# Transposed output projection with router logits beside it, first expert started after half a gather, and one-block weight tiles first in the ring

## The chip, the core and the metric

The kernel runs on one core of a Trainium2 chip. The metric is the device time of one execution in microseconds (us), taken as the median of several runs. Traces and pages of the profile come from one execution recorded by the hardware profiler.

## The reference

One transformer block on 256 tokens of width 1024, all in float32. A mixer (a gated linear recurrence, a differential attention and a sliding-window attention, merged by gates) is followed by a mixture of 32 experts, of which each token takes 4. The part that matters here runs from the merged mixer output to the first expert:

```python
merged = jnp.einsum('bsnd,bsnd->bsd', gates, branch_proj)
return merged @ w_out                                   # output projection, 1024 x 1024
...
x = x + g_m * hybrid_mixer(h, ...)                      # residual
h = rms_norm(x, norm_ffn[layer]) * (1.0 + sc_f) + sh_f
...
logits = xt.astype(jnp.float32) @ w_router.astype(jnp.float32) + b_router.astype(jnp.float32)
top_v, top_e = lax.top_k(logits, TOP_K)
weights = jax.nn.softmax(top_v, axis=-1).astype(xt.dtype)
...
def expert_block(args):
    tok, e = args
    hcat = x_pad[tok] @ w1[e] + b1[e]                   # 1024 -> 2048
    ...
    return act @ w2[e] + b2[e]                          # 1024 -> 1024
```

The weights of the 32 experts are 32 x 12 MB; everything else that is read is small beside them.

## The kernel before

**Stages.** The mixer's branches come first, then `merge` (L621), `project` (L671, the product with `w_out`), `route` (L721, logits, top 4, ranks of the tokens within each expert), and `moe` (L1092), which loops over the experts. An expert takes the tokens chosen for it (at most 64) as columns: `gather` (L865) makes, for four experts at a time, the 1024 x 256 tile `xT` by products of the scaled residual with a one-hot matrix `sel`; `up` (L916) multiplies `xT` by `w1`; `activate`, `down` (L932) and `scatter` follow. The order is up(0), then for each next expert up(e), activate(e-1), down(e-1).

**Weights.** All weights pass through a ring of tiles that SyncE (SP) loads in program order. A *block* is 128 x 2048 float32, 1 MB; the ring of the expert stage has 16 blocks in ten tiles: u0, u1, u2, v0, v1, v2 of two blocks, u3, w0, w1, w2 of one. `slot` (L69) takes the next tile in the list `self.order`; `blocks` (L87) fills a two-block tile by one DMA (L92) and a pair of one-block tiles by two (L96 and L84). A tile is loaded again when the products that read it have ended. While `project` runs, v1, v2 and w2 still hold `w_out`. The order of the ring is set in `mixer`:

```python
self.order = [(wp3, f"u{i}", 2) for i in range(3)] + [o["v0"], o["v1"], (wp3, "u3", 1)] \
    + [o[t] for t in ("w1", "w2", "w0", "v2")]
```

So up(0), which reads eight blocks k = 0..7, reads u0, u1, u2, v0.

**Precision.** The products up to `project` are made of three fast float32r products (`mm3`, L121: high x high, high x low, low x high); `split` (L111) makes the two parts of 128 x 1024 of a weight block, the high one on ScalarE (ACT, L117), the low one on VectorE (DVE, L109), in three buffers. Logits, transposes and expert products are plain float32.

**project and route_half.** `project` makes the output rows by tokens: the merged tile `m` is the stationary operand, `w_out` moves, 512 columns at a time; 48 products for each half of the 1024 columns. DVE multiplies by the row tile `gmB` (the mixer gate copied to all partitions by 8 products at L669) and adds to `x`. `route_half` (L699) then squares `x` on ACT for the norm, transposes the half of `x` by 8 PE transposes, copies it to `x1T`, and multiplies it by the router weights (four products of 32 output partitions each, L718). `route` brings the logits back to tokens (L727), scales them by the norm (`rs`), finds the top 4 (L743 to L748), counts by products with triangular ones (L750 to L754) and gets `rank` (L756). `scaled` (L761) makes the high and low part (`xs`) of the normed x, the low part half on DVE, half on ACT and GpSimd (POOL).

**gather.** For each of 8 chunks d of 128 channels: four products of 128 x 256 (two token halves, high and low part, L883) into one half of a PSUM bank, then DVE (even d) or ACT (odd d) scales the result into `xT`.

Two more things move in the change: the row tile `gf` (the second gate, 8 products, made in `project`) and `counts` (L791), whose result `cnti` SP reads into a register (L1022) ahead of the loads that follow in its order.

The order on each engine is made by a list scheduler from the program text; DMA issues are in one SP queue. The engines wait on semaphores.

## Time and profile before

| what | value |
|---|---|
| median of 3 runs | 1236.9 us (1235.44 to 1237.43) |
| the profiled execution | 1238.5 us, of which the span from first to last instruction is 1236.7 us |
| granted TensorE clock, mean | 0.983 of full |
| busy: PE, DVE, ACT, POOL | 1125.8 us (91%), 452.7 us (37%), 259.3 us (21%), 11.0 us (1%) |
| DMA | 470.70 MB, mean 381 GB/s over the span; 414 to 429 GB/s in each slice from 310 us to 1175 us |

How to read it: the span has a first part of some 300 us (mixer and routing) in which PE, DVE and the loads take turns at the limit, and an expert part in which the loads run at one rate almost to the end. Busy shares over the whole span mix the two. A row of the timeline gives start, duration, engine, source line, operation, tiles written and read, and how many instructions are merged in the row; a float32 product shows as two records.

### The profile page before, as it was taken

How to read it: one execution, taken by the hardware profiler on the slowest of the kernel's cores; microseconds unless marked ns; L12 is line 12 of the kernel's file. 1: busy time of each engine (PE TensorE's matmuls, PEld its weight loads, DVE VectorE, ACT ScalarE, POOL GpSimd, SP SyncE). 2: the span in 40 equal slices, each digit the busy share in tenths (PEclk: the TensorE clock that was granted, in tenths of full speed). 3: DMA queues.
4: the chain of work that ended last, by engine and by line, in shares of the span. 5: the costliest groups of instructions: out<-in, count | busy, mean ns of one | idle time of the engine just before them, and what ended most of it. 6: DMA issues, size and time to landing. Idle time of an engine off the chain costs nothing.

```text
span 1236.7 us, 13932 instructions
## 1 busy us (share of the span) xinstructions
PE 1125.8 (91%) x5719; PEld 552.4 (45%) x5720; DVE 452.7 (37%) x892; ACT 259.3 (21%) x446; POOL 11.0 (1%) x19
## 2 busy tenths in 40 slices
PE   5998999998988999998989798979898989798987
PEld 4787989995333334332323242324233323332333
DVE  3477888974123231231213132403131222121232
ACT  4475668444101011100000010101010100100000
POOL 0000000000010000000000000000000000000000
PEclk9998999998999999999999999999999999999999
DMA  9688467885999999999999999999999999999996
GB/s 376 210 288 299 147 218 264 343 325 219 414 417 425 424 424 426 427 426 425 423 429 424 429 424 424 429 424 424 423 427 427 424 426 424 427 426 426 423 403 237
DMA packets 54718, 470.70 MB, mean 381 GB/s; under 512 B 6048, under 2 KB 8152, under 8 KB 21112
## 3 DMA queue, kind: packets, MB, share of 16 engines
q1 hardware_dynamic: 53112, 466.93, 91.9%
q0 software_dynamic: 528, 1.72, 0.4%
q10 hardware_dynamic: 1008, 1.09, 0.3%
q8 instruction: 47, 0.77, 0.3%
q14 instruction: 23, 0.19, 0.0%
HBM read 468.65 MB, written 1.07 MB: 380 GB/s over the span
## 4 chain that ended last, share of the span: by engine, by line
PE 55%; DMA 41%; DVE 2%; ACT 1%; issue 1%; SPq 0%; DVEq 0%; ACTq 0%
DMA wt<-w2h 31%; PE po L923 10%; PE mm L923 9%; PE ps L943 7%; DMA wt<-w1h 7%; PE ps L956 3%; PE mm L124 3%; PE mm L125 3%; PE mm L126 3%; PE ps L883 3%; DMA wada<-wada 2%; PE ps L850 1%; PE po L125 1%; PE po L126 1%; PE po L124 1%; PE ps L420 1%
## 5 line engine op out<-in xcount | busy, mean ns | idle before, releaser
L923 PE MATMUL po<-wt,xT 128*64 128x512 f32 x992 | 335.7, 599 | 29.1 <-DMA wt<-w1h 29.1
L923 PE MATMUL mm<-wt,xT 128*64 128x512 f32 x992 | 331.4, 594 | 0.0
L943 PE MATMUL ps<-wt,act 128*64 128x512 f32 x992 | 234.3, 614 | 43.0 <-DMA wt<-w2h 36.1
L949 DVE TENSOR_TENSOR y<-ps,gf 64x512 f32<-64x512 f32 x62 | 42.7, 689 | 352.2 <-PE ps L943 351.5
L923 PEld LDWEIGHTS po<-wt,xT 128*64 128x64 f32 x992 | 87.8, 136 | 169.3 <-issue 112.7
L943 PEld LDWEIGHTS ps<-wt,act 128*64 128x64 f32 x992 | 72.7, 140 | 190.0 <-issue 133.6
L923 PEld LDWEIGHTS mm<-wt,xT 128*64 128x64 f32 x992 | 93.0, 137 | 132.5 <-issue 130.8
L853 DVE TENSOR_TENSOR g<-ps,b1t 128x512 f32<-128x512 f32 x31 | 21.4, 691 | 242.9 <-PE ps L850 242.9
L109 DVE TENSOR_TENSOR wlo<-wt,whi 128x1024 fp32r<-128x1024 f32 x72 | 85.6, 1192 | 35.6 <-ACT whi L117 34.4
L117 ACT CAST whi<-wt 128x1024 fp32r<-128x1024 f32 x72 | 73.5, 1023 | 74.4 <-PE ps L126 27.7
L927 ACT COPY hg<-po 128x512 f32<-128x512 f32 x31 | 18.1, 585 | 302.3 <-PE po L923 256.2
L126 PE MATMUL mm<-h,wlo 128*128 128x256 f32 x256 | 73.7, 288 | 0.0
L125 PE MATMUL mm<-h,whi 128*128 128x256 f32 x256 | 73.5, 287 | 0.0
L124 PE MATMUL mm<-h,whi 128*128 128x256 f32 x256 | 73.4, 287 | 0.0
L856 ACT ACTIVATE ps<-g 128x512 f32<-128x512 f32 x31 | 18.6, 601 | 219.9 <-DVE g L854 219.9
L956 PE MATMUL ps<-y,swT 128*128 128x512 f32 (+1 forms) x128 | 58.2, 606 | 6.4 <-DVE y L949 6.4
L958 DVE TENSOR_TENSOR x<-x,ps 128x512 f32<-128x512 f32 x64 | 43.8, 687 | 18.9 <-PE ps L956 18.9
L124 PEld LDWEIGHTS mm<-h,whi 128*128 128x128 f32 x256 | 49.1, 192 | 1.4 <-issue 1.3
L125 PEld LDWEIGHTS mm<-h,whi 128*128 128x128 f32 x256 | 49.0, 191 | 1.1 <-issue 1.0
L126 PEld LDWEIGHTS mm<-h,wlo 128*128 128x128 f32 x256 | 49.0, 192 | 1.0 <-issue 1.0
L886 ACT ACTIVATE xT<-ps,B,A 128x256 f32<-128x256 f32 x32 | 17.3, 564 | 139.1 <-PE ps L883 138.7
L206 DVE CUSTOM_DVE_ANT_0 wada<-wada,silu,cols 128x1024 f32<-128x1024 f32 x32 | 40.8, 1275 | 7.8 <-DMA wada<-wada 7.8
(335 smaller groups left out, 1103.7 us busy)
## 6 DMA issues: line engine op xcount, KB each, us to landing
wt<-w1h SPq DMA_DIRECT2D x93, 2048.0 KB, 29.5
wt<-w2h SPq DMA_DIRECT2D x47, 2048.0 KB, 29.5
wt<-w1h SPq DMA_DIRECT2D x70, 1024.0 KB, 29.6
wt<-w2h SPq DMA_DIRECT2D x33, 1024.0 KB, 31.3
wt<-wch SPq DMA_DIRECT2D x16, 1024.0 KB, 6.7
wada<-wada SPq DMA_DIRECT2D x32, 512.0 KB, 4.7
wada<-wad SPq DMA_DIRECT2D x16, 512.0 KB, 9.4
wt<-wqkv SPq DMA_DIRECT2D x8, 896.0 KB, 8.7
```

The source lines that it names most:

```text
L109: eng.tensor_tensor(lo, x, hi.bitcast(F32), op=ALU.subtract)
L117: self.nc.scalar.copy(hi, w)
L124: nc.tensor.matmul(out, lhs[0], rhs[0], start=start, stop=False)
L125: nc.tensor.matmul(out, lhs[0], rhs[1], start=False, stop=False)
L126: nc.tensor.matmul(out, lhs[1], rhs[0], start=False, stop=stop)
L206: nc.vector.tensor_tensor_reduce(out=w, in0=w, in1=self.csb, scale=0.5, scalar=self.col(C_BADA + c), op0=ALU.mult, op1=ALU.add, accum_out= ...
L883: nc.tensor.matmul(p[:, i * 256:(i + 1) * 256], self.xs[j][:, t, d * 128:(d + 1) * 128], sel[:, t], start=(t + j == 0), stop=(t + j == 2))
L923: nc.tensor.matmul(p[64 * hf:64 * hf + 64], xT[:, k, i * CAP:(i + 1) * CAP], w[:, (2 * j + hf) * 512:(2 * j + hf + 1) * 512], start=(k == ...
L943: nc.tensor.matmul(py[rows[hf]], act[:, (k % 4) * 2 + k // 4, :], w[:, (2 * i + hf) * 512:(2 * i + hf + 1) * 512], start=(k == 0), stop=(k ...
L949: nc.vector.tensor_mul(self.y[r, hf], py[r], self.gf[r, hf * 512:(hf + 1) * 512])
L956: nc.tensor.matmul(p, swT[r, i, t * 128:(t + 1) * 128], self.y[r, hf], start=True, stop=True)
L958: nc.vector.tensor_add(self.x[:, t, s], self.x[:, t, s], p)
```

## The change

1. `project` makes the output transposed: `w_out` (laid out anew) is the stationary operand and `m` moves, 256 columns (the tokens) at a time, in 8 chunks of 128 channels with 24 products each. Before each pair of chunks x is transposed (4 transposes, L687 of the new file) and copied to `x1T`; DVE adds the gated chunk to it in one instruction (L698); each chunk has its own logit product (L699). The sum is transposed back (4 for a pair, L704), squared on ACT straight from PSUM (L706) and copied to `x` by DVE (L707). The row tile `gmB` is gone.
2. The low part of the scaled x (`rest`) is made by DVE alone, in four instructions issued behind the one-hot tiles; ACT makes only the four high parts. The weights of the chosen experts (`route_weights`), `counts` and `gf` come behind up(0) in the program.
3. `gather` yields after each pair of chunks. For the first group up(0) runs on PE in the order written: two pairs, blocks k = 0 and 1, a pair, k = 2 and 3, the last pair, the other blocks. The results of the first gather are all scaled by ACT.
4. The ring begins with the one-block tiles w1 and w2: up(0) reads w1, w2, u0, u1, u2.

```diff
@@ mixer
-            self.order = [(wp3, f"u{i}", 2) for i in range(3)] + [o["v0"], o["v1"], (wp3, "u3", 1)] \
-                + [o[t] for t in ("w1", "w2", "w0", "v2")]
+            self.order = [o["w1"], o["w2"]] + [(wp3, f"u{i}", 2) for i in range(3)] \
+                + [o["v0"], o["v1"], (wp3, "u3", 1), o["w0"], o["v2"]]
@@ router_weights
-        self.gmB = self.row_tile("gmB", gm, self.keep2)
@@ project
-        for hf in range(2):
-            s = slice(hf * 512, (hf + 1) * 512)
-            ps = self.proj([self.mm(), self.mm()], m, self.a["wout"][hf])
-            if hf == 0:
-                self.route_open(st)
-            else:
-                self.gf = self.row_tile("gf", self.mod[:, 40:48], self.keep, self.mm)
-            for t in range(2):
-                y = self.keep2.tile([128, 512], F32, name="y", tag="gb", bufs=2)
-                nc.vector.tensor_mul(y, ps[t], self.gmB[:, s])
-                nc.vector.tensor_add(self.x[:, t, s], y, self.x[:, t, s])
-            self.route_half(hf)
...
+        for i, w in enumerate(self.blocks([self.a["wout"][hf] for hf in range(2)])):
+            b = slice(256 * i, 256 * (i + 1))
+            pt = self.ps()
+            for c in range(2):
+                for t in range(2):
+                    nc.tensor.transpose(pt[:, c * 256 + t * 128:c * 256 + (t + 1) * 128],
+                                        self.x[:, t, b.start + c * 128:b.start + (c + 1) * 128], self.ident)
+            nc.scalar.copy(x1T[i], pt.rearrange("p (c m) -> p c m", c=2))
+            p = self.mm()
+            for c in range(2):
+                d, q = 2 * i + c, slice(c * T, (c + 1) * T)
+                hi, lo = self.split(w[:, c * 1024:(c + 1) * 1024])
+                for k in range(8):
+                    s = slice(k * 128, (k + 1) * 128)
+                    self.mm3(p[:, q], (hi[:, s], lo[:, s]), (m[0][:, k], m[1][:, k]), k == 0, k == 7)
+                xT = x1T[i][:, c]
+                nc.vector.scalar_tensor_tensor(xT, p[:, q], self.gm[:, d:d + 1], xT, op0=ALU.mult, op1=ALU.add)
+                nc.tensor.matmul(self.plg[32 * (d % 4):32 * (d % 4) + 32, :T], self.wr[:, d, :], xT,
+                                 start=(d < 4), stop=(d >= 4))
+            pb = self.ps()
+            for t in range(2):
+                for c in range(2):
+                    nc.tensor.transpose(pb[:, t * 256 + c * 128:t * 256 + (c + 1) * 128],
+                                        x1T[i][:, c, t * 128:(t + 1) * 128], self.ident)
+                nc.scalar.activation(sqj, pb[:, t * 256:(t + 1) * 256], AF.Square, accum_out=self.ssp[:, t, i:i + 1])
+            nc.vector.tensor_copy(self.x[:, :, b], pb.rearrange("p (t m) -> p t m", t=2))
@@ route
-        self.scaled(0)
-        self.scaled(1)
+        for hf in (1, 0):
+            for t in range(2):
+                s = slice(hf * 512, (hf + 1) * 512)
+                nc.scalar.mul(self.xs[0][:, t, s], self.x[:, t, s], rs[:, t:t + 1])
...
+    def rest(self, hf):
...
+            self.nc.vector.scalar_tensor_tensor(self.xs[1][:, t, s], self.x[:, t, s], self.rs[:, t:t + 1],
+                                                self.xs[0][:, t, s].bitcast(F32), op0=ALU.mult, op1=ALU.subtract)
@@ gather
         if g == 0:
-            self.route_weights()
+            with self.tc.issue_after(last.ins):
+                self.rest(0)
+                self.rest(1)
...
+    def gather_steps(self, sel, xT, first):
...
-                if i:
+                if i or first:
                     nc.scalar.activation(xT[:, d], p[:, i * 256:(i + 1) * 256], AF.Identity,
                                          bias=self.B2[:, d:d + 1], scale=self.A2[:, d:d + 1])
...
+            yield
@@ up
+        for _ in range(2 if steps else 0):
+            next(steps)
...
+            if steps and k % 2:
+                next(steps, None)
@@ moe
-            up(0)
+            with self.tc.manual_schedule(engines={mybir.EngineType.PE}):
+                up(0, steps)
+            self.route_weights()
             self.counts()
+            self.gf = self.row_tile("gf", self.mod[:, 40:48], self.keep)
```

What stands on the engines, at the three places that matter. First PE within `project`. Before, near the end of the first half (L124 to L126 are the three products of `mm3`, L709 transposes of x, L718 logits of two chunks):

```order
L125 MATMUL mm<-wlo,m_2444 128x512
L709 MATMUL ps<-kst,x 128x128 x4
L126 MATMUL mm<-whi,m_2445 128x512
...
L124 MATMUL po<-whi,m_2444 128x512
L709 MATMUL ps<-kst,x 128x128 x4
L125 MATMUL po<-wlo,m_2444 128x512
...
L718 MATMUL ps<-x1T_2952,wr 32x256 x2
```

Now, between chunks 5 and 6 (L704 transposes back, L687 transposes of x, L699 one logit product):

```order
L126 MATMUL po<-m_2444,wlo 128x256
L704 MATMUL ps<-kst,x1T_2871 128x128
L687 MATMUL ps<-kst,x 128x128 x4
L125 MATMUL mm<-m_2445,whi 128x256
L699 MATMUL ps<-x1T_2871,wr 32x256
L704 MATMUL ps<-kst,x1T_2871 128x128
L126 MATMUL mm<-m_2444,wlo 128x256
```

Float32 work stands between the float32r products after every chunk; in all of `project` 8 lone logit products instead of 4 pairs, and 16 transposes back beside 16 of x (16 before).

Second, PE from the routing to up(0). Before, `gather` interleaves its banks, and all 32 of its products but one product of up(0) come ahead of up(0):

```order
L883 MATMUL ps<-sel,xs_3101 128x256
L923 MATMUL po<-wt,xT 64x512
L883 MATMUL ps<-sel,xs_3100 128x256
...
L883 MATMUL ps<-sel,xs_3101 128x256
L923 MATMUL po<-wt,xT 64x512
L923 MATMUL mm<-wt,xT 64x512 x2
```

Now (the names `xs_3194` and `xs_3195` are the high and the low part; L917 is `up`):

```order
L874 MATMUL ps<-sel,xs_3195 128x256 x2
L917 MATMUL po<-wt,xT 64x512 x2
L917 MATMUL mm<-wt,xT 64x512 x2
L917 MATMUL po<-wt,xT 64x512 x2
L917 MATMUL mm<-wt,xT 64x512 x2
L874 MATMUL ps<-sel,xs_3194 128x256 x2
L874 MATMUL ps<-sel,xs_3195 128x256 x2
L917 MATMUL po<-wt,xT 64x512
L874 MATMUL ps<-sel,xs_3194 128x256 x2
L874 MATMUL ps<-sel,xs_3195 128x256 x2
L917 MATMUL po<-wt,xT 64x512 x2
```

Ahead of the first L917 stand 16 products of the gather, chunk by chunk; behind the blocks k = 0 and 1 come two chunks more, with one product of up(1) among them.

Third, SP's queue from the first expert load. Before:

```order
L84 DMA wt<-w1h 128x2048
L92 DMA wt<-w1h 128x4096
L84 DMA wt<-w1h 128x2048
L92 DMA wt<-w1h 128x4096 x4
L96 DMA wt<-w1h 128x2048 x2
L92 DMA wt<-w1h 128x4096
L1022 TENSOR_LOAD cnti
L1022 ISA x2
L92 DMA wt<-w2h 128x4096 x2
```

Now:

```order
L96 DMA wt<-w1h 128x2048
L92 DMA wt<-w1h 128x4096
L84 DMA wt<-w1h 128x2048
L92 DMA wt<-w1h 128x4096 x4
L84 DMA wt<-w1h 128x2048
L96 DMA wt<-w1h 128x2048
L92 DMA wt<-w1h 128x4096
L1018 TENSOR_LOAD cnti
L1018 ISA x2
L96 DMA wt<-w2h 128x2048
L84 DMA wt<-w2h 128x2048
L92 DMA wt<-w2h 128x4096
```

The first refills of the ring are two of 1 MB (into w1 and w2) where one of 2 MB (into u0) stood; the register load keeps its place ahead of them.

## Rows read from the trace of the kernel before

**Rows 1.** The page's part 4: the chain that ended last, by engine.

```profile
PE 55%; DMA 41%; DVE 2%; ACT 1%; issue 1%; SPq 0%; DVEq 0%; ACTq 0%
```

**Rows 2.** Stretches: us; busy us of PE, PEld, DVE, ACT, POOL; clock; DMA share; GB/s.

```profile
295.00:308.00 13.00, 10.97 (x57) 7.40 (x59) 5.58 (x22) 4.51 (x8) 1.90 (x2) 0.76 0.00 0
308.00:310.00 2.00, 2.00 (x12) 0.72 (x10) 0.00 (x0) 0.00 (x0) 0.00 (x0) 1.00 0.76 156
310.00:312.00 2.00, 2.00 (x13) 0.59 (x10) 0.00 (x0) 0.00 (x0) 0.00 (x0) 1.00 0.85 360
...
400.00:600.00 200.00, 189.15 (x841) 67.78 (x838) 52.01 (x98) 16.90 (x29) 0.00 (x0) 0.99 1.01 426
```

**Rows 3.** Timeline of SP's queue: start us, us, engine line operation tiles count.

```profile
264.69 15.37 SPq L96 DMA_DIRECT2D wt<-w1h  x2
280.10 0.42 SPq L92 DMA_DIRECT2D wt<-w1h  x1
307.88 3.76 SPq L92 DMA_DIRECT2D wt<-w2h  x2
```

**Rows 4.** Timeline of PE in merge and project.

```profile
215.09 2.03 PE L526 MATMUL ps<-kst,gm 128*128 128x128 f32 x16
...
262.71 0.40 PE L124 MATMUL po<-whi,m 128*128 128x512 f32 x1
...
275.77 0.60 PE L709 MATMUL ps<-kst,x 128*128 128x128 f32 x4
276.13 0.48 PE L126 MATMUL mm<-whi,m 128*128 128x512 f32 x1
...
278.60 0.63 PE L718 MATMUL ps<-x1T,wr 128*32 128x256 f32 x4
279.16 0.50 PE L125 MATMUL po<-wlo,m 128*128 128x512 f32 x1
...
287.25 0.40 PE L126 MATMUL mm<-whi,m 128*128 128x512 f32 x1
```

**Rows 5.** Stretches again: the stage before merge.

```profile
202.00:232.00 30.00, 30.00 (x260) 30.00 (x260) 29.80 (x38) 21.72 (x26) 0.00 (x0) 1.00 0.78 264
```

**Rows 6.** Timeline of PE: lone float32 products, and one 24-product chunk of merge.

```profile
193.24 3.62 PE L367 MATMUL ps<-xc,gw 128*128 128x256 f32 x16
...
231.04 0.28 PE L124 MATMUL mm<-br,whi 128*128 128x256 f32 x1
...
233.92 0.28 PE L124 MATMUL po<-br,whi 128*128 128x256 f32 x1
```

**Rows 7.** Timeline of all engines from the logits to up(0).

```profile
293.18 0.41 DVE L743 SCALAR_TENSOR_TENSOR lg<-ps,rs,lgb 128x32 f32<-128x32 f32 x2 [0.20 <-PE ps L727]
293.51 0.74 DVE L772 SCALAR_TENSOR_TENSOR xs<-x,rs,xs 128x512 fp32r<-128x512 f32 x1
...
294.73 0.95 DVE L780 TENSOR_SCALAR nm<-top 128x2 f32<-128x2 f32 x1
...
296.26 0.23 DVE L756 SCALAR_TENSOR_TENSOR rank<-ps,maskb 128x64 f32<-128x64 f32 x1 [0.48 <-PE ps L754]
...
297.33 4.80 PE L883 MATMUL ps<-sel,xs 128*128 128x256 f32 x24 [1.10 <-DVE sel L871]
...
297.64 0.17 DVE L797 CAST cnti<-cnt 1x33 int32<-1x33 f32 x1
...
303.06 1.21 PE L883 MATMUL ps<-sel,xs 128*128 128x256 f32 x8
...
304.21 0.64 PE L923 MATMUL po<-wt,xT 128*64 128x512 f32 x1
```

**Rows 8.** The page's part 5: scaling of one gathered chunk on ACT.

```profile
L886 ACT ACTIVATE xT<-ps,B,A 128x256 f32<-128x256 f32 x32 | 17.3, 564 | 139.1 <-PE ps L883 138.7
```

**Rows 9.** Stretches again: the clock around the gather.

```profile
294.00:301.00 7.00, 3.97 (x22) 3.92 (x23) 5.20 (x23) 3.35 (x6) 2.51 (x2) 0.53 0.01 5
...
302.00:308.00 6.00, 6.00 (x30) 2.55 (x30) 1.08 (x6) 1.63 (x4) 0.00 (x0) 1.00 0.00 0
```

More of the change, by code (lines that the diff above doesn't have):

```diff
@@ L688, in route_open @@
-    def route_open(self, stack):
-        nc = self.nc
-        self.rw = rw = self.pool(stack, "rw", 1)
+        self.rw = rw = self.pool(st, "rw", 1)
         first = self.mix.tile([128, 4, T], F32, name="x1T0", tag="silu")
-        self.x1T = [first[:, :2], first[:, 2:]]
-        self.x1T += [self.keep2.tile([128, 2, T], F32, name="x1T1", tag="act", bufs=2) for _ in range(2)]
-        self.ssp = rw.tile([128, 2, 2], F32, name="ssp")
-        self.sqj = self.keep2.tile([128, 512], F32, name="sqj", tag="ga", bufs=2)
+        x1T = [first[:, :2], first[:, 2:]]
@@ L696, in route_open @@
+        x1T += [self.keep2.tile([128, 2, T], F32, name="x1T1", tag="act", bufs=2) for _ in range(2)]
+        self.ssp = rw.tile([128, 2, 4], F32, name="ssp")
+        sqj = self.keep2.tile([128, 512], F32, name="sqj", tag="ga", bufs=2)[:, :256]
         self.plg = self.ps()
         nc.scalar.activation(self.ssp[:, 0, 0:1], self.eps, AF.Sqrt)
-    def route_half(self, hf):
-        nc = self.nc
-        s = slice(hf * 512, (hf + 1) * 512)
-        pt = [self.ps(), self.ps()]
-        for t in range(2):
-            nc.scalar.activation(self.sqj, self.x[:, t, s], AF.Square, accum_out=self.ssp[:, hf, t:t + 1])
-            tt = slice(t * 128, (t + 1) * 128)
-            for i in range(4):
-                d = 4 * hf + i
-                nc.tensor.transpose(pt[i // 2][:, i % 2 * 256 + t * 128:i % 2 * 256 + (t + 1) * 128],
-                                    self.x[:, t, d * 128:(d + 1) * 128], self.ident)
-        for d2 in range(2):
-            dst = self.x1T[2 * hf + d2].rearrange("p k m -> p (k m)")
-            if d2:
-                nc.scalar.copy(dst, pt[d2])
-            else:
-                nc.vector.tensor_copy(dst, pt[d2])
-        for i in range(4):
-            nc.tensor.matmul(self.plg[32 * i:32 * i + 32, :T], self.wr[:, 4 * hf + i, :],
-                             self.x1T[2 * hf + i // 2][:, i % 2], start=(hf == 0), stop=(hf == 1))
@@ L870, in gather @@
         for t in range(2):
-            nc.vector.tensor_tensor(sel[:, t], iota,
+            last = nc.vector.tensor_tensor(sel[:, t], iota,
                                     self.rank[:, t, 4 * g:4 * g + 4, None].to_broadcast([128, 4, CAP]),
@@ L880, in gather @@
                 d = 2 * d2 + i
-                for t in range(2):
-                    for j in range(2):
+                for j in range(2):
+                    for t in range(2):
                         nc.tensor.matmul(p[:, i * 256:(i + 1) * 256], self.xs[j][:, t, d * 128:(d + 1) * 128],
                                          sel[:, t], start=(t + j == 0), stop=(t + j == 2))
-                if i:
+                if i or first:
                     nc.scalar.activation(xT[:, d], p[:, i * 256:(i + 1) * 256], AF.Identity,
@@ L890, in gather @@
                                             self.B2[:, d:d + 1], op0=ALU.mult, op1=ALU.add)
-        return sel, xT
+            yield
     def scatter(self, g, sel):
@@ L914, in scatter, with up @@
         return swT
-    def up(self, xT, i, e):
+    def up(self, xT, i, e, steps=None):
         nc = self.nc
+        for _ in range(2 if steps else 0):
+            next(steps)
         pg, pl = self.mm(), self.mm()
@@ L1097, in moe, with up @@
             sel, xT, swT, h, act = {}, {}, {}, {}, {}
-            sel[0], xT[0] = self.gather(0)
-            def up(e):
+            sel[0], xT[0], steps = self.gather(0)
+            def up(e, steps=None):
                 g, i = divmod(e, 4)
-                h[e] = self.up(xT[g], i, e)
+                h[e] = self.up(xT[g], i, e, steps)
             def gather(g):
                 if g < NE // 4:
-                    sel[g], xT[g] = self.gather(g)
+                    sel[g], xT[g], steps = self.gather(g)
+                    for _ in steps:
+                        pass
             def activate(e):
```

20 lines of the change are left out of this document (6 added, 14 removed).

## The prediction

> **What bounds it now.** I read the chain of waits first: it is made of PE and DMA and of next to nothing else [rows 1]. The reader should then ask which of the two holds in which stage, and the stretches tell it [rows 2]. From 400 to 600 us the DMA share is 1.01 at 426 GB/s: the expert stage goes at the rate of the loads, and PE, though 189.15 of 200 us busy, follows them. From 295 to 308 us the DMA share is 0.00. The queue of SP shows why [rows 3]: two loads given at 264.69 fill its list until 280.10, the rest of the ring goes out behind them, and the next issue comes only at 307.88, when up(0) has ended its products with u0. In between the ring is full and no weight moves. So every microsecond by which that first refill comes earlier or later moves all of the expert stage, and the end, with it. The restart is not sharp: 156 GB/s in 308 to 310 us, 360 in the next two. These 1.03 MB, where 426 GB/s for the 4.12 us since 307.88 would be 1.76, cost (0.73 MB)/(426 GB/s) = 1.7 us. This price is paid each time an idle queue starts.
>
> The path to that refill runs through merge and project (PE), the routing (DVE and PE in turns), the gather and two blocks of up(0). The forecast is the sum of the changes along this path, and of what the new order of the ring does to the restart.
>
> **A, ahead of project: -0.9.** The row tile gmB, 2.03 us of PE until the next work [rows 4], goes: -1.8 without what overlaps. The first four transposes of x come in its place, 0.36 (275.77 to 276.13, rows 4): -1.4. But DVE, which makes the low parts of the weights, is busy 29.80 of the 30 us from 202 to 232 [rows 5], so PE may only wait longer for them. Bounds -1.4 and 0; I take a value nearer to the gain, since behind 232 us PE sets the pace.
>
> **B, project: +6.7.** It now takes 24.8 us (262.71 to 287.25 and the last product's end, rows 4).
> - Float32r products: 96 of 512 columns become 192 of 256. Merge shows these: 24 starts in 2.88 us, 0.120 each [rows 6], 23.0 us; today's take 0.234 each (24.54 from the first start to the last, less 2.3 of other work inside, over 95), 22.4, of which a little is lost in the switches already counted: +0.3 to +0.6, and I take +0.3.
> - Logits: two products into different groups of 32 columns of the array take 0.56 together (four records, 278.60 to 279.16, rows 4), so they run beside one another; there are two such pairs in project, 2 x 0.63 = 1.3, and the other four come behind it. Now seven of eight lie inside it, each alone. The nearest row of lone float32 products of 256 columns is L367: 16 records, 8 products, in 3.62 [rows 6], 0.45 each, and 0.41 without the tail of the last one. With 0.13 for the switch of type there and back (the 0.63 of the pair less its 0.56, twice), 7 x 0.54 less 1.3 is +2.5. If they were cheap beside the others, only the switch, 7 x 0.13, would be left.
> - Transposes: 12 of x and 12 back inside it, at 0.09 (0.36 for four), 2.2, and six switches, 0.8, against 2 x 0.36 before: +2.2.
> - Waits: a lone logit product stands in PE's list behind DVE's addition, and the transposes back behind both. DVE is also making low parts (half of a chunk's weights each), so an addition can be late by up to about 1 us; over seven chunks I put 1.5, and 0.5 for the chunks of m that merge ends last, less 0.3 of today's: +1.7 (bounds 0 and +3.5). Queued behind it on PE are the float32r products of the next chunk, which have no other engine to take them.
> The bounds are +3.7 (waits nil, half of the logits' price) and +8.5. With A, project ends at about 293.3 instead of 287.5.
>
> **C, from project's end to the first refill: -5.1.** Today 287.5 to 307.88 is 20.4 us.
> - End to the logits' `lg` (293.18) [rows 7]: 5.7. The two additions, the squares, 8 transposes, the copies and 4 logits become one addition, one logit, 4 transposes, 2 squares: 4.6, bounds 4.0 and 5.7, since squares and back transposes share one bank.
> - `lg` to `rank` (296.26): 3.1. `xs` (0.74) and `nm` (0.95, stretched by POOL's work) leave DVE's list or shrink: 1.6.
> - `rank` to up(0) (304.21): 7.95. Today 32 gather products, 24 in 4.80 and 8 in 1.21, part of them at a granted clock of 0.53 (294 to 301) [rows 9], the lower level of 1.2 GHz; 1.00 from 302 on. PE had been waiting on DVE's routing steps when it fell. Now 16 products lead, but the low parts stand behind `sel` on DVE, two of 0.74 before the first chunk can end, and each scaling on ACT, 0.56 [rows 8], holds the bank that the next chunk of the pair would write: 6.8.
> - up(0) to the issue: 3.7 for two blocks. One block is half of the 3.45 that two take at full clock, 1.72, and the same lag to the issue, 0.25, and 0.3 for the clock: 2.3.
> Together 15.3 instead of 20.4. Bounds -6.5 (lg at 4.0, scaling hidden) and -3.4 (5.7 and a late second chunk). The first refill comes at 293.3 + 15.3 = 308.6, against 307.88: what the half gather gains, project has spent.
>
> **D, the shape of the refill: +2.4.** Today the first refill is 2 MB, and the next block pair follows 3.45 us later, before the 4.9 us that 2 MB take at 426 GB/s are over: the queue never empties. Now w1 gives 1 MB at R and w2 1 MB at R + 1.7, which are through at R + 1.7 + 4.9 = R + 6.6. The next release is u0's, at R + 7.2: 1.72 for block 1, 1.1 for the pair of gather chunks behind it (8 products in 1.21, less what overlaps), 0.9 for the product of up(1) and the switch, 3.45 for u0. The queue would be dry for 0.6 to 0.7 and pay the restart, 1.7, a second time. Bounds 0 (the products of up(1) lie elsewhere, so it stays fed) and +2.4, which I take, because 6.6 against 7.2 is the working with all of the rows. The Trainium skill, "DMA: Bandwidth & Descriptors", section "Anatomy of one DMA — SWDGE (gpsimd) path", gives a fixed cost of about 2.0 us for each DMA beside its bytes; these loads are SP's and not GpSimd's, and no run so far shows a lone 1 MB. By that price D would be 0.7 + 2.0 = 2.7, and the sum 0.3 higher, 1240.3.
>
> **Nothing.** The cast `cnti` at 297.64 stood 10 us ahead of the first refill and its register load is SP's next step; with `counts` behind up(0) in the program it has some 4 us left, hidden by the wait for w1, and adds one for one if late, with every refill queued behind it on SP. The products of `gf` now lie behind up(0), hidden by DMA's pace. The loads ahead of 293 us keep their order but for names.
>
> **Sum.** -0.9 + 6.7 - 5.1 + 2.4 = +3.1, of which the second restart is the part without which the change is near nothing. The profiled execution took 1238.5 us (span 1236.7), 1.6 above the median of the runs; the sum is made on its span, where it gives 1239.8 and 1241.6 for that execution, and carried to the median: 1236.9 + 3.1 = **1240.0 us**. All lower bounds of the terms give 1236.9 - 4.2 = 1232.7; all upper ones 1236.9 + 7.5 = 1244.4.
>
> **Rivals.**
> - The queue does not run dry (D = 0): +0.7, 1237.6. For it: 0.6 us is little, and a faster gather pair closes the gap. Against it: PE's order has a product of up(1) and all of the pair ahead of u0's blocks.
> - The other side: PE takes the inserted float32 work cheaply. Logit products cost little beside the float32r ones, only their switch 0.13, and no wait: B is about +2.1 (0.3 + 0.9 - 1.3 + 2.2), the sum -1.5, 1235.4; with a queue that stays fed too, 1233.0. For it: pairs of logits ran beside each other in 0.56. Against it: the row of lone ones, 0.41, and DVE's part in every chunk. It decides once B is below +3.6, for then the sum is under zero.
> - Half clock reaches into up(0): PE rests in the routing as today (granted 0.53), and with 16 instead of 32 gather products ahead, block 0 is taken at 1.2 GHz: 1.72 more, 1241.7. For it: the rows at 0.53 last until about 301, some 3.7 us into the gather, and the new lead of 16 products is shorter than that. Against it: the new products are spread by waits over as long a time.
> - The start of the stream doesn't set the end, or the terms cancel: 1236.9. Against it: the DMA share of 1.01 over the whole expert stage.
>
> **How the numbers follow.** Forecast 0.38 (own range 1237.9 to 1242.1), fed queue 0.18, cheap float32 0.22, half clock 0.14, no effect 0.08. A measurement of this kernel can tell about 0.2%, 2.5 us, from no change: the bounds are 1234.4 and 1239.4. Faster: nearly half of the cheap case and a little of the fed queue, 0.13. Same: the rest of the cheap case 0.12, most of the fed queue 0.13, no effect 0.08 and the lower part of the forecast 0.10, 0.43. Slower: the rest, 0.44. The range 1234.0 to 1243.0 leaves out the fastest part of the cheap case (some 0.1) and the worst of the half-clock case with the waits (0.08).
>
> **What would show it.** Project's length should be 31 to 32 us (first project product to the last); a length under 28.5 speaks for the cheap case, and lone L699 products should take some 0.4. From project's end to `lg` 4 to 5.7; from `rank` to up(0) about 6.8; the first refill within 1 us of 308.6. In the stretches, a dip of the DMA share some 7 us behind the first refill, which the fed queue would not show; the granted clock in the first block. The tail should be as long as before, and the rate 426 GB/s. The prediction is wrong if the first refill comes before 306 or after 311, or if the end does not follow it one for one.

## The result and the profile after

The changed kernel takes 1246.83 us in the median of 4 runs (1244.75 to 1248.36), the kernel before 1237.16 in 4 runs beside it: ratio 1.0077, 95% interval [1.0064, 1.009], so it is slower by 0.8%, 9.7 us. A second set of 6 runs gave 1246.51 us and 1.0071 [1.005, 1.0092]. The forecast was 1240.0 with a range to 1243.0: the sign came out as forecast, the size did not. The sign is little to its credit, since it had given 0.44 to slower and 0.43 to no difference. The profiled execution took 1245.68 us, its span 1243.9, 7.2 above the span before; the other 2.5 us are in how the two profiled executions stand to their medians.

The first time to look at is that of the refill of the ring. SP's queue in the timeline (start us, us, operation, tiles, count), which answers to [rows 3]:

```profile
283.70 0.33 SPq L84 DMA_DIRECT2D wt<-w1h  x1
284.12 0.38 SPq L96 DMA_DIRECT2D wt<-w1h  x1
284.55 0.42 SPq L92 DMA_DIRECT2D wt<-w1h  x1
311.01 0.33 SPq L96 DMA_DIRECT2D wt<-w2h  x1
312.73 0.33 SPq L84 DMA_DIRECT2D wt<-w2h  x1
318.65 0.33 SPq L92 DMA_DIRECT2D wt<-w2h  x1
324.31 13.85 SPq L92 DMA_DIRECT2D wt<-w1h  x4
```

The first refill is 3.1 us later than the 307.88 of before, and the third comes 7.6 us behind the first. What the loads make of that is in the stretches (us; busy us of PE, PEld, DVE, ACT, POOL; clock; DMA share; GB/s), which answer to [rows 2, 9]:

```profile
296.00:300.00 4.00, 0.61 (x8) 0.29 (x7) 2.20 (x14) 2.52 (x6) 0.00 (x0) 0.62 0.00 0
300.00:307.00 7.00, 4.79 (x15) 3.60 (x16) 5.11 (x20) 4.31 (x8) 0.00 (x0) 0.50 0.01 2
307.00:311.00 4.00, 4.00 (x13) 1.42 (x14) 0.00 (x0) 0.56 (x1) 0.00 (x0) 0.55 0.00 0
311.00:313.00 2.00, 2.00 (x11) 0.67 (x8) 0.00 (x0) 0.00 (x0) 0.00 (x0) 1.00 0.52 123
313.00:317.00 4.00, 4.00 (x20) 1.65 (x20) 0.00 (x0) 1.13 (x2) 0.00 (x0) 1.00 0.98 373
317.00:319.00 2.00, 2.00 (x11) 0.75 (x8) 0.00 (x0) 0.00 (x0) 0.00 (x0) 1.00 0.43 180
319.00:321.00 2.00, 2.00 (x15) 1.50 (x15) 0.00 (x0) 0.84 (x2) 0.00 (x0) 1.00 0.81 172
325.00:327.00 2.00, 2.00 (x12) 0.68 (x10) 0.00 (x0) 0.11 (x1) 0.00 (x0) 1.00 1.05 287
400.00:600.00 200.00, 188.45 (x842) 66.83 (x840) 51.76 (x98) 18.60 (x32) 0.00 (x0) 0.98 1.01 426
```

Three things stand there: the clock is at its lower level (0.50, 1.2 GHz) from the routing to 311 us, through the first block of up(0); the stream sinks to 172 to 180 GB/s at 317 to 321 us, and to 287 at 325; and from 400 to 600 us it has the same 426 GB/s as before. The same stretch from the first refill to 350 us, first before, then after, gives the size of the second:

```profile
307.88:350.00 42.12, 42.12 (x193) 14.90 (x191) 7.45 (x18) 5.30 (x8) 0.00 (x0) 1.00 0.99 409
```

```profile
311.01:350.00 38.99, 38.99 (x189) 15.14 (x186) 5.74 (x16) 8.63 (x14) 0.00 (x0) 1.00 0.93 359
```

I call *lag* the time that the stream has lost by 350 us against 425.5 GB/s (the rate of the expert stage, 425 to 426 in both traces) from the first refill on: 42.12 x (1 - 409/425.5) = 1.6 us before, 38.99 x (1 - 359/425.5) = 6.1 after. First refill plus lag is where a stream without losses would have begun: 309.5 and 317.1 us. What is left of the span behind it, 927.2 and 926.8, is the same; over all traces of this study it lies between 926.8 and 929.1. So the whole loss lies ahead of 350 us. The path, all times in us, by starts of instructions:

| piece | before | forecast | after | after, second trace |
|---|---|---|---|---|
| first product of project | 262.7 | 261.8 | 261.9 | 261.8 |
| project, first to last product | 24.5 | 31.2 | 31.6 | 31.6 |
| last product to `lg` | 5.9 | 4.8 | 4.8 | 4.8 |
| `lg` to `rank` | 3.1 | 1.6 | 1.7 | 1.7 |
| `rank` to the first refill | 11.6 | 9.1 | 11.05 | 11.06 |
| lag | 1.6 | 4.0 | 6.1 | 6.0 |

The forecast was right down to `rank`, and wrong in the last two rows, in both traces by the same amounts. The timeline between `rank` and up(0) shows the first of them (names as in the order above: `xs` low parts on DVE, L877 the scaling):

```profile
299.96 0.23 DVE L747 SCALAR_TENSOR_TENSOR rank<-ps,maskb 128x64 f32<-128x64 f32 x1 [0.48 <-PE ps L745]
300.22 0.76 DVE L855 TENSOR_TENSOR sel<-kst,rank 128x256 fp32r<-128x256 f32 x2
300.80 2.15 PE L874 MATMUL ps<-sel,xs 128*128 128x256 f32 x4 [0.87 <-ACT xs L727]
300.90 2.73 DVE L756 SCALAR_TENSOR_TENSOR xs<-x,rs,xs 128x512 fp32r<-128x512 f32 x4
302.98 0.56 ACT L877 ACTIVATE xT<-ps,B,A 128x256 f32<-128x256 f32 x1 [0.55 <-PE ps L874]
303.60 2.08 PE L874 MATMUL ps<-sel,xs 128*128 128x256 f32 x8 [0.66 <-ACT xT L877]
306.34 1.22 PE L874 MATMUL ps<-sel,xs 128*128 128x256 f32 x4 [0.66 <-ACT xT L877]
307.49 1.98 PE L917 MATMUL po<-wt,xT 128*64 128x512 f32 x4
309.25 1.71 PE L917 MATMUL mm<-wt,xT 128*64 128x512 f32 x4
```

Sixteen products take from 300.80 to 307.49, 6.7 us, where 24 of before took 4.80 [rows 7]: the first chunk waits for two low parts, the next ones for the scaling in their bank (the waits of 0.66), at half clock (0.50); and the first block takes 3.31 us (307.49 to 310.80), where half of the 3.45 that two blocks take at full clock is 1.72.

Project itself is as it was worked out. PE's instructions from 261.9 to 293.8 us in groups (line, operation, tiles, count | busy us, mean ns | idle before, releaser; five more groups of project's float32r products and two lone products of merge are left out):

```profile
L126 PE MATMUL mm<-m,wlo 128*128 128x256 f32 x32 | 9.2, 288 | 0.3 <-DVE wlo L109 0.3
L699 PE MATMUL ps<-x1T,wr 128*32 128x256 f32 x14 | 4.3, 391 | 0.7 <-DVE x1T L698 0.7
L704 PE MATMUL ps<-kst,x1T 128*128 128x128 f32 x13 | 3.2, 286 | 0.0
L687 PE MATMUL ps<-kst,x 128*128 128x128 f32 x12 | 1.8, 272 | 0.0
```

PE's waits are 1.0 us in all (0.3 and 0.7; the groups left out have none), so of the 7.1 us that project gained in length, some 6.1 are work and switches.

### The profile page after: what moved, and what is told of

It is laid out like the page before. It is cut to its first block, busy times and chain, and to the rows that moved or that the text cites. A ratio compares the mean times of both kernels' runs of the same rounds, so it can differ in the third digit from the quotient of the medians.

```text
span 1243.9 us, 14134 instructions
## 1 busy us (share of the span) xinstructions
PE 1136.0 (91%) x5815; PEld 559.1 (45%) x5816; DVE 451.4 (36%) x892; ACT 261.6 (21%) x456; POOL 8.5 (1%) x17
## 3 DMA queue, kind: packets, MB, share of 16 engines
q0 software_dynamic: 528, 1.72, 0.4%
## 4 chain that ended last, share of the span: by engine, by line
PE 49%; DMA 44%; DVE 3%; ACT 2%; issue 1%; SPq 1%; DVEq 0%; ACTq 0%
DMA wt<-w2h 40%; PE po L917 9%; PE mm L917 8%; PE ps L939 7%; PE ps L952 3%; PE mm L124 3%; PE mm L126 3%; PE mm L125 3%; DMA wt<-w1h 2%; DMA wada<-wada 2%; PE po L124 1%; PE po L126 1%; PE po L125 1%; PE ps L874 1%; PE ps L834 1%
## 5 line engine op out<-in xcount | busy, mean ns | idle before, releaser
L917 PE MATMUL po<-wt,xT 128*64 128x512 f32 x992 | 319.1, 606 | 36.6 <-DMA wt<-w1h 36.6
L917 PE MATMUL mm<-wt,xT 128*64 128x512 f32 x992 | 316.6, 600 | 0.0
L939 PE MATMUL ps<-wt,act 128*64 128x512 f32 x992 | 231.5, 611 | 29.9 <-DMA wt<-w2h 25.0
L917 PEld LDWEIGHTS po<-wt,xT 128*64 128x64 f32 x992 | 80.7, 137 | 173.0 <-issue 104.0
L917 PEld LDWEIGHTS mm<-wt,xT 128*64 128x64 f32 x992 | 86.6, 138 | 134.4 <-issue 132.7
L124 PE MATMUL mm<-h,whi 128*128 128x256 f32 x256 | 73.6, 287 | 0.9 <-ACT gl L617 0.9
L126 PE MATMUL mm<-h,wlo 128*128 128x256 f32 x256 | 73.7, 288 | 0.0
L124 PEld LDWEIGHTS mm<-h,whi 128*128 128x128 f32 x256 | 49.1, 192 | 2.5 <-issue 1.3
L126 PEld LDWEIGHTS mm<-h,wlo 128*128 128x128 f32 x256 | 49.0, 191 | 1.0 <-issue 1.0
L877 ACT ACTIVATE xT<-ps,B,A 128x256 f32<-128x256 f32 x36 | 19.7, 564 | 136.2 <-PE ps L874 136.0
```

The lines of the kernel that those rows point to most:

```text
L124: nc.tensor.matmul(out, lhs[0], rhs[0], start=start, stop=False)
L126: nc.tensor.matmul(out, lhs[1], rhs[0], start=False, stop=stop)
L917: nc.tensor.matmul(p[64 * hf:64 * hf + 64], xT[:, k, i * CAP:(i + 1) * CAP], w[:, (2 * j + hf) * 512:(2 * j + hf + 1) * 512], start=(k == ...
L939: nc.tensor.matmul(py[rows[hf]], act[:, (k % 4) * 2 + k // 4, :], w[:, (2 * i + hf) * 512:(2 * i + hf + 1) * 512], start=(k == 0), stop=(k ...
```

## The experiments

Every ratio is to the kernel before, run beside it on the same chip (medians of 1238.0 to 1238.8 us in 21 to 25 runs). A ratio is not the quotient of the two medians and differs from it by up to 0.0010, 1.2 us. In most expectations Theory 1 takes the time to be the path to the first refill plus the lag behind it.

**old_project** undoes the transposed project (and the layout of `w_out`, gmB, the routing by halves); **proj_only** is its complement, the kernel before with `project` of the change and `gf` behind up(0).

```diff
@@ old_project: the changed kernel, project
-        for i, w in enumerate(self.blocks([self.a["wout"][hf] for hf in range(2)])):
...
+        for hf in range(2):
+            s = slice(hf * 512, (hf + 1) * 512)
+            ps = self.proj([self.mm(), self.mm()], m, self.a["wout"][hf])
...
+            self.route_half(hf)
@@ proj_only: the kernel before, project and moe
-            ps = self.proj([self.mm(), self.mm()], m, self.a["wout"][hf])
...
+        for i, w in enumerate(self.blocks([self.a["wout"][hf] for hf in range(2)])):
...
             self.counts()
+            self.gf = self.row_tile("gf", self.mod[:, 40:48], self.keep)
```

> The changed kernel with project, the half-wise routing of it, gmB and the layout of w_out as before; the late low parts, the half gather and the new ring stay. Theory 1: project ends 6 us earlier, the logits come 1.2 later behind it, the rest is as in the changed kernel: -4.8, 1242 us, still slower than before by about 5 us (half clock in block 0 and dry queue). Rival (the transposed project is the whole of the loss): 1236 to 1237 us, as before or faster.

Measured: 1240.74 us, 1.0023 [1.0012, 1.0034]. So the transposed project costs about 6 us within the change (1246.5 to 1246.8 less 1240.7), where 4.8 were expected here, and the rest by itself still 2.8 by the ratio, 1.9 by the medians. Its trace has the first refill at 304.06, but a lag of 6.3:

```profile
304.06 0.33 SPq L96 DMA_DIRECT2D wt<-w2h  x1
305.78 0.33 SPq L84 DMA_DIRECT2D wt<-w2h  x1
311.70 0.33 SPq L92 DMA_DIRECT2D wt<-w2h  x1
317.34 13.85 SPq L92 DMA_DIRECT2D wt<-w1h  x4
```

> The kernel before with the transposed project alone (and gf's products behind up(0), where the change puts them). Theory 1: project 7 us longer (31.6), the logits 1.1 us sooner behind it, routing and gather as before: +6, 1244.5 us. Rival (what project loses comes from its meeting with the other parts): within 2 us of before.

Measured: 1246.51 us, 1.0068 [1.0055, 1.0081], 8.4 us, 2 more than its longer project explains, and as slow as the whole change. Its lag is 1.7, as before; what grew is `rank` to the first refill, 14.2 us instead of 11.6. Against the routing, `x` comes later there, so POOL's share of the low parts falls on `sel`:

```profile
300.09 2.67 POOL L759 TENSOR_TENSOR xs<-xsv,xs 128x512 fp32r<-128x512 f32 x2 [44.43 <-DVE maskb L737]
300.75 2.29 DVE L860 TENSOR_TENSOR sel<-kst,rank 128x256 fp32r<-128x256 f32 x2
303.19 5.18 PE L872 MATMUL ps<-sel,xs 128*128 128x256 f32 x22 [0.64 <-DVE cnt L784]
```

`sel` takes 2.29 us beside POOL, against 1.00 before, where the two overlap less, and 0.76 in the changed kernel, where POOL does nothing, and the bulk of the gather starts 2.7 us behind `rank` instead of 1.1. The Trainium skill, "SBUF — State Buffer", section "SBUF: two separate sides", says that such an instruction of DVE and one of POOL lock each other out of a pair of ports they share; the row agrees. So the two parts are not additive: the rest of the change costs 2.8 us with the old project and nothing that shows with the new one. That it is the low parts' move to DVE which pays there is read from this row, and was not tried apart.

**proj_only_warm** and **before_warm** put products on PE that nobody reads (fillers), to tell the clock from waits: in both

```diff
+        warm = self.mm()
+        for _ in range(6):
+            nc.tensor.matmul(warm[:, :T], lgT[:, :128], lgT, start=True, stop=True)
...
+            for _ in range(2):
+                nc.tensor.matmul(warm[:, :T], lgT[:, :128], lgT, start=True, stop=True)
```

the six behind the products that bring the logits back to tokens, the two behind the counting products.

> proj_only (the kernel before with the transposed project) with 8 products of 256 columns on PE that nobody reads, 6 between the logits and the counting products and 2 behind those. Theory 1 (proj_only lost 2 us more than its longer project explains, because the half clock lasted 11 us there against 7.4 in the trace of before): the granted clock stays near 1.00 and the time falls by 2 to 3 us, to 1244 us or a little under. Rival (the 2 us are waits of the gather for DVE and ACT): 1246.5 as proj_only.

Measured: 1247.25 us, 1.008 [1.0058, 1.0102]: no gain. The clock was 0.58 from 300 to 308 all the same, and `lg` came 0.5 later behind project. In the trace `rank` to the first refill is 12.7 us instead of 14.2, but the median shows nothing of it, so this run does not tell the two theories apart. `sel` took 2.31 us again in it.

> The kernel before with the same 8 products. Theory 1: the half clock from 293.5 to 301 us goes, and with it about half of the 4.8 us of the first 24 gather products: -1 to -2, 1236.5 us. Rival: no change, 1238.2.

Measured: 1236.34 us (12 runs), 0.9981 [0.9968, 0.9995]: 2.3 us faster by the ratio, 1.7 by the medians, and the lowest median and ratio of the study, ahead of both kernels compared here. Here the clock held:

```profile
295.00:305.00 10.00, 9.83 (x56) 5.84 (x56) 4.36 (x20) 3.09 (x7) 0.56 (x1) 1.00 0.00 0
```

against 0.53 in 294 to 301 us [rows 9]; `rank` to the first refill is 9.9 us instead of 11.6 (294.89 to 304.83).

**warm** does the same in the changed kernel: 7 behind the logits, 2 behind the counting, and 21 short ones where the first half of the gather pauses.

```diff
@@ warm: gather_steps
                 for j in range(2):
+                    for _ in range((6 if d == 0 and j else 5 if d and not j else 0) if first and d < 4 else 0):
+                        nc.tensor.matmul(wf[:, :256], sel[:, 0, :2].rearrange("p e c -> p (e c)"),
+                                         sel[:, 0].rearrange("p e c -> p (e c)"), start=True, stop=True)
```

> The changed kernel with products on PE whose results nobody reads: 7 of 256 columns while DVE finds the top 4, 2 behind the counting products, 21 of one pass in the pauses of the first half of the gather. Theory 1 (half clock from the routing reaches through the gather and block 0 and costs 2 to 2.5 us): the granted clock stays at or near 1.00 from 296 to 311 us, up(0)'s first block takes 1.7 us instead of 3.3 and the first refill comes 2 to 3 us earlier in its distance from project: 1244.5 us. Rival (the pauses are waits for DVE and ACT, and the clock costs nothing there): the clock rises, the time stays at 1246.8; if the fillers hold up the counting products, up to +1.

Measured: 1244.5 us, 1.005 [1.0032, 1.0067], 2.0 to 2.3 us less than the change's two sets. The two stretches on either side of the gather's end:

```profile
302.00:308.00 6.00, 5.83 (x41) 4.73 (x39) 4.45 (x18) 3.77 (x7) 0.00 (x0) 1.00 0.01 3
308.00:310.00 2.00, 2.00 (x11) 0.73 (x12) 0.00 (x0) 0.56 (x1) 0.00 (x0) 1.00 0.00 0
```

`rank` to the first refill is 8.5 us there (301.40 to 309.94), 2.5 less, and the lag is 6.0, as without them. The clock is thus worth 2.5 us of that piece, more than the 1.9 that the forecast had missed in it; `lg` comes 0.5 later behind project there, which leaves the 2.0 to 2.3 of the median.

**two_halves** moves the second half of the gather behind block 3, and **banks** also sends the chunks through two banks in turn (0, 2, 1, 3), scaled by DVE and ACT in turn:

```diff
@@ two_halves: up
-            if steps and k % 2:
-                next(steps, None)
+            if steps and k == 3:
+                for _ in steps:
+                    pass
@@ banks: gather_steps
-        for d2 in range(4):
-            p = self.ps()
-            for i in range(2):
+        for d4 in range(2):
+            pp = [self.ps(), self.ps()]
+            for i, c in ((0, 0), (0, 1), (1, 0), (1, 1)):
...
-                if i or first:
+                if c:
```

> The changed kernel with the second half of the gather in one piece behind the blocks k = 0 to 3, instead of a pair of chunks behind every two blocks. Theory 1 (the end is the first refill plus the lag of the stream behind it): the first refill stays where it is (some 49 us behind project's first product), but u0's release comes 5.2 us behind it, before the two 1 MB refills are through, and the lag falls from about 6.1 to about 3 us: -3, 1243.8 us. Rival (the lag is the price of the two 1 MB loads, not of the late release): no change.

Measured: 1246.53 us, 1.006 [1.0037, 1.0082]; the lag is 5.8. The rival's number came, no change, but not by its reason alone: u0's release moved up, and the pause moved on to u1's:

```profile
312.90 0.33 SPq L96 DMA_DIRECT2D wt<-w2h  x1
314.62 0.33 SPq L84 DMA_DIRECT2D wt<-w2h  x1
318.05 0.33 SPq L92 DMA_DIRECT2D wt<-w2h  x1
325.84 13.85 SPq L92 DMA_DIRECT2D wt<-w1h  x4
```

4 MB given by 318.05 last, by an estimate with the restart of 1.7 and 426 GB/s, until 312.90 + 1.7 + 9.8 = 324.4, and 325.84 is late again: 16 products, with one of up(1) and three of `gf` between them, took 4.2 us on PE (317.93 to 322.14).

> As two_halves, and in each half the chunks go in turn through two banks (chunks 0, 2, 1, 3), scaled by DVE and ACT in turn, so that no chunk waits for the scaling of the one before it. Theory 1: the four waits of 0.66 to 0.87 us between chunks on PE go, and block 0 starts about 1.5 us earlier, so another -1.5 against two_halves, 1242.3 us. Rival (DVE's low parts set the pace of the first half, not the bank): within 0.4 us of two_halves.

Measured: 1243.03 us (12 runs), 1.0041 [1.0029, 1.0054], 3.5 less than two_halves where 1.5 were expected: the first refill comes 8.7 us behind `rank` (299.32 to 308.03) instead of 11.05, and as the second half is shorter too, the lag falls to 4.3.

```profile
300.15 3.01 PE L876 MATMUL ps<-sel,xs 128*128 128x256 f32 x8 [0.87 <-ACT xs L727]
303.50 2.08 PE L876 MATMUL ps<-sel,xs 128*128 128x256 f32 x8 [0.34 <-DVE xT L882]
305.50 1.62 PE L919 MATMUL po<-wt,xT 128*64 128x512 f32 x4
306.96 1.03 PE L919 MATMUL mm<-wt,xT 128*64 128x512 f32 x4
```

Of the 2.3 us, 1.3 are shorter pauses: `rank` to up(0) is 6.2 instead of 7.5. The other 1.0 is the clock, which was 0.50 up to 306.5 and 1.00 from 307 on: block 0 takes 2.3 us (305.50 to 307.82) instead of 3.3. So the pauses and the clock are not two separate costs; with the pauses shortened the clock was back about 3 us sooner behind `rank`.

**whole_gather** takes all of the gather ahead of up(0), **old_ring** puts back the ring's old order, **new_ring** puts the new order into the kernel before.

```diff
@@ whole_gather: up
-        for _ in range(2 if steps else 0):
+        for _ in range(4 if steps else 0):
@@ old_ring: mixer (new_ring: the reverse, in the kernel before)
-            self.order = [o["w1"], o["w2"]] + [(wp3, f"u{i}", 2) for i in range(3)] \
-                + [o["v0"], o["v1"], (wp3, "u3", 1), o["w0"], o["v2"]]
+            self.order = [(wp3, f"u{i}", 2) for i in range(3)] + [o["v0"], o["v1"], (wp3, "u3", 1)] \
+                + [o[t] for t in ("w1", "w2", "w0", "v2")]
```

> The changed kernel with all of the first gather ahead of up(0). Theory 1: the first refill comes 4 to 5 us later less about 1.3, as block 0 is then at full clock, +3.3; the dry stretches (about 4 us) go; sum -0.7 (-2 to +1), 1246 us. Rival (half of the gather ahead is worth what it moves, since the start alone counts): +3.3, 1250 us.

Measured: 1246.91 us, 1.0075 [1.006, 1.009], as the change itself: `rank` to the first refill grew from 11.05 to 15.2, the lag fell from 6.1 to 2.5. What the half gather gains at the start it loses behind it, within 0.6 us. In the kernel before the whole gather leads as well, and there `rank` to up(0) is 7.95 us, here 13.2 (298.63 to 311.88; clock 0.50 from 299 to 311, and 0.66 of waiting between chunks). So the way in which the change makes the gather costs some 5.3 us ahead of up(0), nearly all of the 5.7 that are saved by starting behind half of it (7.5).

> The changed kernel with the old order of the ring (u0 first), all else as changed. Theory 1 (the time is the start of the stream plus the stretches in which the queue then runs dry): in the changed kernel the two 1 MB refills go at 311.0 and 312.7 us, and the next releases come at 318.7 and 324.3, so the queue empties before each. With u0 first the first refill is 2 MB at about 312.7, through at 319.3, so u1's release at 318.7 comes in time: the start is 1.7 us later, the dry stretch at 317 to 320 us is gone, the sum is -1 (-2.5 to +0.5), 1246 us. Rival (the order of the one-block tiles costs all of what I called D, 4 us, and nothing is paid for the later start): 1242.5 us.

Measured: 1247.38 us, 1.0074 [1.006, 1.0089], no difference from the change that these runs could tell, and the rival's 1242.5 is out; the lag is 4.3, 1.8 less, and the first refill 1.5 later from `rank`.

> The kernel before with the new order of the ring alone. Theory 1: up(0) follows the whole gather here without a break, so w1 is free 1.7 us earlier than u0 was (306.2 instead of 307.9), w2 1.7 later, u0 at 311.3, before the 2 MB are through (312.8): no dry stretch, -1.7, 1235.4 us. Rival (loads of 1 MB are in themselves slower to start, about 1.7 us of restart each): +1.7, 1239 us.

Measured: 1237.64 us (11 runs), 0.9994 [0.9983, 1.0004]. Taken as changes, the -1.7 of Theory 1 lies inside the interval (-2.1 to +0.5 us) near its edge, the rival's +1.7 outside it; the middle is -0.7. The first refill came only 0.7 us sooner behind `rank` (10.9 instead of 11.6). Nothing was late here (refills at 304.25, 305.96, 309.40, 312.83), and yet the lag is 3.3:

```profile
304.00:306.00 2.00, 2.00 (x12) 0.72 (x10) 0.00 (x0) 0.00 (x0) 0.00 (x0) 1.00 0.41 78
306.00:308.00 2.00, 2.00 (x12) 0.66 (x10) 0.00 (x0) 0.00 (x0) 0.00 (x0) 1.00 0.93 348
308.00:310.00 2.00, 2.00 (x12) 0.63 (x10) 0.00 (x0) 0.00 (x0) 0.00 (x0) 1.00 1.03 324
310.00:312.00 2.00, 2.00 (x12) 0.72 (x10) 0.00 (x0) 0.00 (x0) 0.00 (x0) 1.00 1.18 422
312.00:314.00 2.00, 2.00 (x12) 0.65 (x10) 0.00 (x0) 0.00 (x0) 0.00 (x0) 1.00 0.87 279
314.00:316.00 2.00, 2.00 (x10) 0.49 (x6) 0.00 (x0) 0.53 (x1) 0.00 (x0) 1.00 0.92 369
```

So this stream, which starts on single megabytes, is at 279 to 369 GB/s in four of the five steps from 306 to 316 us and at 422 in the fifth; at 324 GB/s the DMA share is 1.03, so an idle queue is not the reason there. The lag is 1.7 us more than before here, 0.9 more in whole_gather. That eats what the order gains by starting sooner. The Trainium skill, "DMA: Bandwidth & Descriptors", section "Anatomy of one DMA — SWDGE (gpsimd) path", gives a fixed cost of about 2.0 us for a DMA of GpSimd's; these loads are SP's. Taken over as an estimate it would have added 2.0 for the one load more; both traces lie under it.

**logits_grouped** makes four logit products together behind chunks 3 and 7.

```diff
@@ logits_grouped: project
-                nc.tensor.matmul(self.plg[32 * (d % 4):32 * (d % 4) + 32, :T], self.wr[:, d, :], xT,
-                                 start=(d < 4), stop=(d >= 4))
+            for d in range(4 * (i // 2), 4 * (i // 2) + 4) if i % 2 else ():
+                nc.tensor.matmul(self.plg[32 * (d % 4):32 * (d % 4) + 32, :T], self.wr[:, d, :],
+                                 x1T[d // 2][:, d % 2], start=(d < 4), stop=(d >= 4))
```

> The changed kernel with the logit products of four chunks made together, in the four column groups, behind chunks 3 and 7, instead of one behind each chunk. Theory 1 (lone logits cost 0.55 us each with the switch, and PE waits 0.7 us for DVE before the one of chunk 6): project to its last product some 2.5 to 3.5 us shorter, 28 to 29 us; the four behind chunk 7 take 0.2 to 0.6 longer than the one did: -2.5, 1244 us. Rival (they cost only their columns, the group of four as much as four lone ones): no change.

Measured: 1245.94 us, 1.0063 [1.005, 1.0076]. Project is 30.0 us, 1.6 shorter, about half of what was expected, and the time about 1 us less, which the intervals do not tell from none. The group behind chunk 7 was not kept together on PE: 286.46 has two of them, 290.11 and 290.92 one each.

**old_proj_banks** puts old_project and banks together; **opb_warm** adds fillers (3, 2 and 12), **best_cold** the old order of the ring instead, **best** fillers to that (7, 2 and 12).

> The changed kernel with project as before (as in old_project), and the gather in two halves through two banks (as in banks). Theory 1: the terms add up: 1240.7 - 3 - 1.5 = 1236.2 us, 2.6 below the kernel before. Rival (with the earlier project the gains of the gather overlap with it): 1238 to 1239, no better than before.

Measured: 1237.68 us (11 runs), 0.9997 [0.9985, 1.001], the same as before. Its first refill is at 303.72, 39.9 us behind project's first product (45.2 before), but 3 of these 5.3 us go into a lag of 4.6, and the other 2.3 do not show in the median. In its trace project begins 1.1 us later than before, and what follows the lag is 0.8 longer.

> As old_proj_banks (project as before, gather in two halves through two banks) with the old order of the ring, u0 first. Theory 1 (the stream's lag is set by how far the loads given run ahead of the queue): the first refill is 1.7 to 2 us later than there, but it is 2 MB with 2 MB more 3.4 us behind it, and the lag falls from 4.6 to 1.6 to 2 us: -1, 1236.7 us. Rival (the early 1 MB is worth its 1.7 us): +1.7, 1239.4 us.

Measured: 1239.63 us (12 runs), 1.0015 [1.0004, 1.0027]. The rival held: first refill 3.1 us later from project, of which 1.7 is the second block, lag only 1.3 less.

> As best_cold, with products on PE that nobody reads in the pauses of the routing and of the first half of the gather, so that the clock stays up. Theory 1: gather and the first blocks at full clock, 1.5 to 2.5 us off the first refill: 1234.5 to 1235 us, 3.5 below before. Rival (the pauses of PE set the distance, not the clock): as best_cold.

Measured: 1240.92 us (12 runs), 1.0022 [1.0012, 1.0032], no gain. The clock was at 1.00, but the 7 fillers held up the counting products: `lg` to `rank` 3.2 us instead of 1.7.

> old_proj_banks (project as before, gather in two halves through two banks, new ring) with products that nobody reads: 3 ahead of the counting products (so that these are not held up, as the 7 of best did by 1.5 us), 2 behind them, 12 short ones in the pauses of the first half of the gather. Theory 1: first half of the gather and block 0 at full clock, -2 against old_proj_banks: 1235.5 to 1236 us, 2 to 3 below before. Rival (the clock had already come back ahead of block 0 there, so the fillers only cost): 1237.7 or above.

Measured: 1236.69 us (12 runs), 0.9996 [0.9982, 1.0009]. That lies between the two numbers expected. With 3 fillers `rank` was in time and the clock at full, but the first refill came only 0.6 sooner behind project's first product than in old_proj_banks, and the lag stayed at 4.7.

> The changed kernel itself, once more, with a second trace. Theory 1: 1246.5 to 1247 us; from rank to the first refill 11 us as in its first trace, the lag of the stream again about 6 us, since both come from waits and releases that are fixed by the program. Rival (these two were peculiar to one execution): the two terms differ by over 1 us from the first trace.

Measured: 1246.51 us; both terms as in the first trace (the table above). So they are not peculiar to the first execution.

## Why the prediction was wrong

- *What bounds it*: right. In each of the traces the span is the first refill, its lag, and 926.8 to 929.1 us; the chain of the page has gone from 41 to 44% DMA:

```profile
PE 49%; DMA 44%; DVE 3%; ACT 2%; issue 1%; SPq 1%; DVEq 0%; ACTq 0%
```

- *A, -0.9*: not tested. Project begins 0.8 us earlier in the trace after, but over the traces of this study it begins anywhere from 258.3 to 263.8 us, with and without gmB.
- *B, +6.7*: right, 7.1 measured. Within it the waits were smaller (1.0, put at 1.7) and so the products and switches dearer (6.1, put at 5.0); undoing it gave about 6 us. The rival of cheap float32 work falls, and grouping the logits gives back only 1.6.
- *C, -5.1*: failed in its second half. The steps to `lg` and `rank` came within 0.1 us. But "`rank` to up(0) 6.8" and "up(0) to the issue 2.3", 9.1 together, took 11.05. The step that failed is the clock: I had let it come back as before and put 0.3 for it. It stayed at 0.50 through the half gather and nearly all of block 0, so that `rank` to up(0) took 7.5 and up(0) to the issue 3.5; with it held up (warm) the piece is 6.6 + 2.0 = 8.5, near the 6.8 + 2.3 that I had put. That case stood as a rival with a chance of 0.14 and a price of 1.7 us, and it is the one that came. banks shows that shorter pauses bring the clock back sooner, so the clock and the waits of the gather fail together.
- *D, +2.4*: right in kind, too small: 4.5. I counted one dry stretch, up to u0's release (R + 7.2, measured 7.6). The next release, u1's, comes 5.7 us behind it, more than the 4.9 that 2 MB last, since every pair of blocks had a pair of chunks and its waits ahead of it: the stream sank at 317 to 321, and again at 325. And the order with single megabytes first lost 0.9 to 1.7 us even where nothing was late (whole_gather, new_ring); why is open.
- *Nothing*: not quite so. Three of the eight products of `gf` stand inside up(0) (0.83 us at 319.12), between the last two chunks of the gather, and not behind it; what they cost there was not tried.
- Together +0.4, +1.9 and +2.1 are 4.4 us, and the span's 7.2 is 4.1 above the forecast's 3.1. The rest of the 9.7, 2.5 us, is the place of two profiled executions in their spreads; I had carried the sum to a median of 3 runs that was 1.1 to 1.9 us below the later, longer sets, and that part of it is no effect of the change. In the second set the medians are 8.5 us apart, beside 23 runs of the kernel before.
- The head start of the half gather, the change's gain, is real (5.7 us from `rank` to up(0) against whole_gather) and is spent twice: the slower making of the gather takes 5.3 of it, so that 0.6 are left at the first refill, and the lag grows by 4.5.

## What to carry to other kernels

Where a stream of loads sets the end, count from the first refill not only its time but the bytes given and the time of each release after it: a release that comes sooner but alone is worth nothing if the next one is late. Splitting a stage in order to start its successor sooner puts the rest of the stage into that successor, and here each piece of it came back as a pause of the stream. And where a change leaves PE less work between its waits, look at the granted clock in the stretch behind.

## What the runs showed of the hardware

- The lower clock outlasts its cause: PE was busy 0.61 of 4 us from 296 to 300, and the clock was at 0.50 until 310.5, about 10 us behind the first product of the gather; in banks it was there until 306.5, about 6 us behind it, and in the kernel before until 301, about 4. Products without a use took 2.3 us off the kernel before (0.9981 [0.9968, 0.9995]); in best, where they stood ahead of the counting products, they cost 1.5 us between `lg` and `rank`.
- An instruction of DVE beside one of POOL: `sel` 2.29 us for two (proj_only), against 0.76 without it (the change).
- A restart on single megabytes: 348, 324, 422, 279 and 369 GB/s in steps of 2 us in new_ring, with every load given before the ones ahead of it were through, against 426 GB/s later. Why such a stream is slower was not settled; no run gave the same bytes in other pieces at the same times.
